# Attention pieces in three steps instead of two: transposes and their copy, then the next scores, then the older product

## The chip, the core and the metric

One NeuronCore of a Trainium2 chip runs one program. Its engines work side by side and wait for each other by semaphores: TensorE (PE in the profile, its weight loads PEld), VectorE (DVE), ScalarE (ACT), GpSimd (POOL) and SyncE (SP, which issues the DMAs). Each engine works off a queue of its own. The metric is the device time of one execution in microseconds (us).

## What is computed

Two transformer blocks, one after the other. The first has two layers over two streams, 256 context and 256 latent tokens of 1024 channels; each layer is a feed-forward part, a mixer (differential attention beside a Fourier mixer, merged by gates) and a second feed-forward part. The second block (gated delta rule, mLSTM, experts) is not touched here. The part that matters is the attention of the first block:

```python
def diff_attend(q, k, v, lam):
    s = jnp.einsum("bqhcd,bkhcd->bhcqk", q, k).astype(jnp.float32) * (HEAD_DIM ** -0.5)
    p = jax.nn.softmax(s, axis=-1)
    a = p[:, :, 0] - lam * p[:, :, 1]
    return jnp.einsum("bhqk,bkhe->bqhe", a.astype(v.dtype), v)
```

There are 8 heads. Each has two score maps c of 64 channels, whose softmaxes are subtracted, and values of 128 channels. Context tokens attend to the 256 context keys, latent tokens to all 512 keys. The last layer computes latent queries alone.

## The kernel before

Matrix products are made of three products each, of high and low halves (mm3, L169 to L171), to keep float32's precision; the weights arrive by DMA as "wraw" and are split on ScalarE and VectorE into "whi" and "wlo" (L140, L141). Such products of weights and tokens are called "pg" in the mixer.

Attention goes by pieces of 128 queries of one head. Layer 0 has 32 pieces, in the order of the heads and, within a head, two context pieces (256 keys) and two latent ones (512 keys). Layer 1 has 16, all of 512 keys. The method `attend` (L527) is a generator; a piece does the following:

- scores: six matmuls into two accumulators "psc" (one for each c)
- softmax: on VectorE the two maxima (L540), on ScalarE the two exponentials "e" with their sums (L542), on VectorE the reciprocal (L544), the scaling (L545) and the difference of the two maps (L546, which writes "e" again). Here the generator yields
- transposes: one for each 128 keys into "pT" on TensorE (L550), with a copy to "aT" by ScalarE (L552)
- the values' product: one matmul for each 128 keys into "po" (L555; the trace shows two records for each) and a copy to "o" by ScalarE (L557).

In the loop of `mixer` (L663 to L680) a piece's first part is recorded, then the rest of the piece before. When a head's last piece is through, `head_done` squares its output ("sqo", ScalarE) and sums it on TensorE into "pst"; after heads 1 and 3 it also records the projections of the next queries and keys (`pair`), and the gates' projections are recorded behind the loop, each held back behind a "pst" (`issue_after`, L683). These projections are the "pg" matmuls that the scheduler puts between the steps of the pieces; they are called fillers below. `split_qk` splits the next head's queries and keys into halves ("qh", "kh" on ScalarE, "ql", "kl" on VectorE).

What is recorded goes through a scheduler. It fills the queue of each engine one instruction at a time, with the earliest recorded one that it takes to be ready at that point; so what stands where between the pieces is its doing, and a change in the order of recording moves fillers and splits too. Buffers set limits: the accumulators "psc", "pT", "po" and "pst" share four ("pa"), the fillers' four others ("ps").

Of the kernel before, what the change touches and what calls it, by code (L numbers as in the profile page):

```python
# [35 lines left out]
class Kernel:  # L36
    def __init__(self, ctx, tc, A, NW=4, NTMP=6):
# [21 lines left out]
        # ones in column s  # L59
# [4 lines left out]
        # picks row 32 g + s into column 2 g + s  # L64
# [6 lines left out]
        # adds the rows 32 g + s into column s  # L71
# [3 lines left out]
    def block(self, n, nch):  # L75
        """Pools of one of the two blocks."""
        st = ExitStack()
        self.act = st.enter_context(self.tc.tile_pool(name=f"act{n}", bufs=nch, reuse_waits="tile"))
        self.bp = st.enter_context(self.tc.tile_pool(name=f"blk{n}", bufs=1, reuse_waits="tile"))
        return st  # L80

    # ---- tiles
# [15 lines left out]
    # ---- small parameters as columns [128, rows]  # L98
# [23 lines left out]
    # ---- weights: raw -> (hi, lo), both exact in float32r  # L122
    def weights(self, src, k0, nk, c0, ncol=256, nsplit=2, half=None):
# [7 lines left out]
        with ExitStack() as order:  # L131
            # the second weights after a norm are not split ahead of it
# [11 lines left out]
    def weights_parts(self, srcs, n):  # L144
        """For several [src, first column] of 8 x 128 rows, 256 columns: their (hi, lo), and functions that load and split the i-th of
        n parts of the rows of each."""
# [26 lines left out]
    # ---- adaLN vectors  # L173
# [10 lines left out]
    def ada(self, cm, wsrc, i, bias, out, streams=(0, 1)):  # L184
        """(A generator; its second step is best taken some time after the first.) out [128, NK, 2] =
        silu(c) @ w[:, i-th D columns] + bias columns, the products on DVE, summed over the partitions on PE."""
# [36 lines left out]
    def ada_quarter(self, cm, ws, q, bias, out):  # L223
        """The channels of the q-th 256 of such a vector, the products on PE, for both streams."""
# [17 lines left out]
    # ---- statistics over the model dimension  # L242
    def square(self, c, s, xt, scales=(None,)):
        """Adds (x * scale)^2 of the chunk c of stream s to the sums of its tokens, for each of scales."""
# [10 lines left out]
    def sums(self, s, i=0):  # L255
        """[128, 256] PSUM (all partitions alike): those sums over the model dimension."""
        pt = self.pa("pst")[:, :S]
        self.nc.tensor.matmul(pt, self.ones, self.sq.pop((s, i)), start=True, stop=True)
        return pt

    def rsqrt_table(self, t):
        """Has the table of rsqrt loaded ahead of its use, once t is there."""
# [5 lines left out]
    def rsqrt(self, sums, n, tag="rs", k=1):  # L268
        """rsqrt(sums / n + k eps), k 1, 4 or eps: the engine's estimate with one Newton step."""
# [16 lines left out]
    def modulated(self, x, gs, sh, streams):  # L286
        """(x * rstd * gs + sh) split into hi, lo; gs, sh [128, NK, 2]."""
# [9 lines left out]
    def norm_part(self, U, x, gs, sh, s, r, cs):  # L297
        """The chunks cs of the stream s of it, into U."""
# [13 lines left out]
    def scale_cols(self, g, sc, name):  # L312
        """g * (1 + scale): [128, NK, 2]."""
# [16 lines left out]
    def ffn(self, x, U, w_in, w_out, gate, streams, fill=lambda end=False: None, scales=(None,), fills=(), head=None):  # L330
# [3 lines left out]
        for a in range(0, nchunk, 8):  # L334
            b = min(a + 8, nchunk)
            H = []
            for j in range(a, b, 2):
# [14 lines left out]
                if j == 0 and head is not None:  # L352
                    begin, end = head(U, load, split)
                    wdma = self.wdma
                    # the vectors' products run ahead of the others by a quarter
# [46 lines left out]
    def load_x(self):  # L402
        """The streams as 8 tiles [128 channels, 256 tokens] each; self.r: their rstd."""
# [33 lines left out]
    # ---- attention / Fourier mixer  # L437
    def mixer_consts(self):
        nc = self.nc
        # ones in column h of the h-th block  # L440
# [20 lines left out]
    def gemm_t(self, src, U, nk, c0, nchunk, sl, done, first=False, tail=(), half=None):  # L461
        """done(m, psum) for each 128-column chunk of src[:, c0:], as [columns, tokens] of the slice sl;
        for the last two chunks done(m, psum, part) for each part of tail."""
# [25 lines left out]
    def gemm_rows(self, src, U, c0, ncol, toks, done, first=False):  # L489
        """done(t, c, psum[:, :256]) for each 128 tokens x 256 columns, as [tokens, columns]."""  # L490
# [36 lines left out]
    def attend(self, h, Q, K, V, lam, q0, nkeys, out):  # L527
        """out [128 e, 128 q] <- head h of the queries from q0 on, keys 0..nkeys; Q, K: its hi, lo."""
# [23 lines left out]
        nc.scalar.copy(aT, pT)  # L552
        po = self.pa("po")[:, :128]
# [5 lines left out]
    def mixer(self, x, U, l, last, lam_init, gcol, bg, gate, fill=lambda end=False: None):  # L559
        """gcol: subln_g column; bg: b_gate columns [128, 16]; gate: [128, NK, 2]."""  # L560
# [50 lines left out]
        # Fourier mixing  # L611
# [5 lines left out]
        # cosines of the frequencies 0..128, sines of 1..127: the others' are these, the sines negated  # L617
# [19 lines left out]
        def gdone(dst, m0):  # L637
            def done(m, p):
                t = self.ch(name="gate")
                # sigmoid(z) = (tanh(z / 2) + 1) / 2, the half taken with w_o's gate  # L640
# [21 lines left out]
        prev = ahead = None  # L662
        for h in range(8):  # L663
# [4 lines left out]
            for s in qstreams:  # L668
                for q0 in (s * S, s * S + 128):
                    u = self.attend(h, *halves, V, lam, q0, T if s == LAT else S, o[:, q0:q0 + 128])  # L670
                    next(u)
                    if prev:
                        next(prev[0], None)
                        if prev[1] is not None:
                            head_done(*prev[1])
                    prev = (u, (h, o) if (s, q0) == (LAT, S + 128) else None)
                    if (s, q0) == (LAT, S) and h + 1 < len(Q):
                        ahead = split_qk(h + 1)
        next(prev[0], None)
        head_done(*prev[1])  # L680
# [39 lines left out]
    # ---- second block: mixer  # L720
# [21 lines left out]
    def final_and_mod(self, X, gs, sh):  # L742
        """hi, lo of the modulated norm of rms_norm(X, fg); gs: its gain, times fg."""
        nc = self.nc
        sq = [self.sq.pop((LAT, i)) for i in range(2)]
        # rsqrt(mean(x1^2) + eps) of x1 = X fg rsqrt(mean(X^2) + eps), times the latter:
        # rsqrt(mean((X fg)^2) + eps (mean(X^2) + eps))
# [11 lines left out]
    def final_norm(self, X, fg, sq):  # L759
        """(A generator of two steps.) X <- rms_norm(X, fg), in place; sq: the sums of its squares by partition."""  # L760
# [8 lines left out]
    def block2_consts(self):  # L769
        nc, A = self.nc, self.A  # L770
        c = self.bp
        # the last to be read lie first
        self.OA, self.OB = (c.tile([128, 2, 8, 64], F32, name="O" + n) for n in "AB")
        self.sqn = c.tile([128, 2, 8], F32, name="sqn")
        # strictly later (fwd) and strictly earlier (rev): [j, i]
# [8 lines left out]
        # per gate row: bias, sign, coefficient  # L784
# [18 lines left out]
    def gate_rows(self, U):  # L803
        """The gates' projections and what the recurrences need of them."""
# [1115 lines left out]
```

## Time and profile before

| | us |
|---|---|
| median of 3 runs | 2866.65 |
| lowest and highest run | 2863.99, 2866.95 |
| span of the profiled execution, first to last instruction | 2863.3 |
| attention stretch of layer 0 (615.1 to 767.6) | 152.5 |
| attention stretch of layer 1 (1789.9 to 1893.9) | 104.0 |

The profiled execution has a span of its own; a run's time is a little more, since it also holds what lies around the span. A start in the rows is counted from the span's start. A matmul's duration overlaps the next one's start, so the cost of one in a row of equals is the distance of two starts. Idle time before an instruction stands in square brackets in a timeline, with the instruction that ended it.

### The profile page before, as it was taken

To read this page: it belongs to the slowest core of one execution; us is meant where nothing else is said; L and a number is where in the kernel's file an instruction comes from. 1 tells how busy PE (TensorE), PEld (TensorE's weight loads), DVE (VectorE), ACT (ScalarE), POOL (GpSimd) and SP (SyncE) were. 2 spreads that over 40 slices of the span, in tenths; PEclk is the share of its full clock that TensorE was granted. 3 is DMA by queue.
4 is the path that set the end of the run, shared out by engine and by line. 5 is a ranking of instruction groups with operands and counts; after the bars stand their busy time and mean duration, and the time that the engine had idled before them with its cause. 6 is when DMAs were issued, how large, how long until landed. Compare 5 with 4: busy or idle time off the path is not lost. (4 is left out here: it accounts for less than half of the span.)

```text
span 2863.3 us, 39743 instructions
## 1 busy us (share of the span) xinstructions
PE 2776.7 (97%) x16186; PEld 2266.0 (79%) x16186; DVE 1726.5 (60%) x2974; ACT 1089.8 (38%) x1994; POOL 28.4 (1%) x97
## 2 busy tenths in 40 slices
PE   8999999999999999999999999999998999999997
PEld 6787789876778777788777899779998898895443
DVE  5855675357558656665464565866567865564332
ACT  4222243335624222242222344555446555543222
POOL 0000000000000000000000000000000100000000
PEclk9999999999999999999999999999999999999999
DMA  7644444131123446436464454234555320159997
GB/s 253 207 146 162 145 146 156 63 105 45 45 89 133 162 147 209 168 126 202 154 215 151 149 172 143 74 104 162 177 175 159 102 74 23 33 192 341 366 366 251
DMA packets 354695, 450.27 MB, mean 157 GB/s; under 512 B 13919, under 2 KB 319945, under 8 KB 354505
## 3 DMA queue, kind: packets, MB, share of 16 engines
q1 hardware_dynamic: 352489, 442.42, 46.8%
q0 software_dynamic: 864, 3.15, 0.3%
q8 instruction: 129, 2.11, 0.3%
q10 hardware_dynamic: 1152, 2.10, 0.2%
q14 instruction: 61, 0.50, 0.1%
HBM read 446.57 MB, written 1.05 MB: 156 GB/s over the span
## 5 line engine op out<-in xcount | busy, mean ns | idle before, releaser
L140 ACT CAST whi<-wraw 128x1024 fp32r<-128x1024 f32 (+2 forms) x476 | 466.1, 1005 | 724.7 <-PE py L170 220.8
L141 DVE TENSOR_TENSOR wlo<-wraw,whi 128x1024 fp32r<-128x1024 f32 (+2 forms) x476 | 548.8, 1168 | 254.2 <-ACT whi L140 251.9
L169 PE MATMUL pab<-uh,whi 128*128 128x512 f32 (+1 forms) x1472 | 527.1, 362 | 8.4 <-ACT uh L307 8.4
L171 PE MATMUL pab<-uh,wlo 128*128 128x512 f32 (+1 forms) x1472 | 528.9, 360 | 0.9 <-DVE wlo L141 0.9
L170 PE MATMUL pab<-ul,whi 128*128 128x512 f32 (+1 forms) x1472 | 529.6, 361 | 0.0
L169 PEld LDWEIGHTS pab<-uh,whi 128*128 128x128 f32 x1472 | 276.9, 190 | 60.5 <-ACT uh L307 9.3
L171 PEld LDWEIGHTS pab<-uh,wlo 128*128 128x128 f32 x1472 | 278.8, 190 | 46.7 <-DVE wlo L141 1.6
L170 PEld LDWEIGHTS pab<-ul,whi 128*128 128x128 f32 x1472 | 279.1, 190 | 44.4 <-DVE ul L308 0.4
L198 DVE SCALAR_TENSOR_TENSOR part<-wada,cm,part 128x1024 f32<-128x1024 f32 x238 | 292.6, 1283 | 19.9 <-DMA wada<-in_ada_w_dram 10.8
L171 PE MATMUL pg<-uh,wlo 128*128 128x256 f32 (+1 forms) x864 | 285.6, 331 | 2.3 <-DVE wlo L141 2.3
L169 PE MATMUL pg<-uh,whi 128*128 128x256 f32 (+1 forms) x864 | 286.2, 332 | 1.5 <-ACT cvo L888 0.9
L170 PE MATMUL pg<-ul,whi 128*128 128x256 f32 (+1 forms) x864 | 285.1, 330 | 0.0
L170 PE MATMUL py<-hl,whi 128*128 128x512 f32 (+1 forms) x740 | 265.1, 358 | 0.1
L169 PE MATMUL py<-hh,whi 128*128 128x512 f32 (+1 forms) x740 | 264.7, 358 | 0.0
L171 PE MATMUL py<-hh,wlo 128*128 128x512 f32 (+1 forms) x740 | 263.7, 357 | 0.0
L169 PEld LDWEIGHTS pg<-uh,whi 128*128 128x128 f32 x864 | 165.6, 192 | 20.4 <-issue 2.8
L171 PEld LDWEIGHTS pg<-uh,wlo 128*128 128x128 f32 x864 | 165.4, 192 | 19.7 <-issue 3.7
L170 PEld LDWEIGHTS pg<-ul,whi 128*128 128x128 f32 x864 | 165.8, 192 | 14.6 <-issue 1.9
L169 PEld LDWEIGHTS py<-hh,whi 128*128 128x128 f32 x740 | 139.0, 188 | 23.8 <-issue 1.2
L170 PEld LDWEIGHTS py<-hl,whi 128*128 128x128 f32 x740 | 139.2, 188 | 22.7 <-DVE hl L380 0.3
L171 PEld LDWEIGHTS py<-hh,wlo 128*128 128x128 f32 x740 | 139.1, 188 | 22.7 <-issue 0.4
L377 DVE TENSOR_TENSOR silu<-silu,pab 128x512 f32<-128x512 f32 (+1 forms) x88 | 54.3, 620 | 144.5 <-PE pab L171 144.3
(494 smaller groups left out, 4233.4 us busy)
## 6 DMA issues: line engine op xcount, KB each, us to landing
wraw<-in_ffn_w_in_dram SPq DMA_DIRECT2D x86, 1024.0 KB
wraw<-in_w_in_dram SPq DMA_DIRECT2D x68, 1024.0 KB
wada<-in_w_mod_dram SPq DMA_DIRECT2D x64, 1024.0 KB
wraw<-in_ffn_w_out_dram SPq DMA_DIRECT2D x32, 1024.0 KB
wm<-in_w_gate_dram SPq DMA_DIRECT2D x61, 512.0 KB
wm<-in_w_up_dram SPq DMA_DIRECT2D x61, 512.0 KB
wm<-in_w_down_dram SPq DMA_DIRECT2D x30, 1024.0 KB
wada<-in_ada_w_dram SPq DMA_DIRECT2D x24, 1024.0 KB
```

Of the source, the lines that this page charges most:

```text
L140: nc.scalar.copy(hi[:, a:b], raw[:, a:b])
L141: nc.vector.tensor_tensor(lo[:, a:b], raw[:, a:b], f32(hi[:, a:b]), op=OP.subtract)
L169: nc.tensor.matmul(ps, wh, uh, start=first, stop=False)
L170: nc.tensor.matmul(ps, wh, ul, start=False, stop=False)
L171: return nc.tensor.matmul(ps, wl, uh, start=False, stop=last)
L198: nc.vector.scalar_tensor_tensor(p, w[:, k], c, p, op0=OP.mult, op1=OP.add)
L377: nc.vector.tensor_tensor(t[:, sl], t[:, sl], P[2 + i], op=OP.mult)
```

## The change

The generator yields a second time, between the copy "aT" and the values' product. The loop keeps a list of pieces that are not through. For each new piece it first records the transposes and the copy of the piece before it, then the new piece's scores and softmax, then the product of the piece before last. At the end of the layer the last transposes are recorded and the products that are left. Comments are taken out elsewhere, so lines behind L552 have a number one higher, and behind the loop nine higher.

```diff
@@ attend
         aT = self.tmp(name="aT")[:, :nkeys]
         nc.scalar.copy(aT, pT)
+        yield
         po = self.pa("po")[:, :128]
...
@@ mixer
-        prev = ahead = None
+
+        ahead, pieces = None, []
+
+        def third():
+            u, end = pieces.pop(0)
+            next(u, None)
+            if end is not None:
+                head_done(*end)
         for h in range(8):
             o = self.ch(name="o")
             O.append(o)
...
                     u = self.attend(h, *halves, V, lam, q0, T if s == LAT else S, o[:, q0:q0 + 128])
+                    if pieces:
+                        next(pieces[-1][0])
                     next(u)
-                    if prev:
-                        next(prev[0], None)
-                        if prev[1] is not None:
-                            head_done(*prev[1])
-                    prev = (u, (h, o) if (s, q0) == (LAT, S + 128) else None)
+                    pieces.append((u, (h, o) if (s, q0) == (LAT, S + 128) else None))
+                    if len(pieces) == 3:
+                        third()
                     if (s, q0) == (LAT, S) and h + 1 < len(Q):
                         ahead = split_qk(h + 1)
-        next(prev[0], None)
-        head_done(*prev[1])
+        next(pieces[-1][0])
+        while pieces:
+            third()
```

The built programs hold the same instructions but for two table loads of ScalarE, which the new order has more, and differ in order in the two attention stretches alone; the DMA issues stand as before. Three places show it. The numbers behind the names tell buffers apart.

TensorE, near the end of layer 1, before: the transposes of a piece, its own product, the next scores.

```order
L169 MATMUL psc_14584<-kh_14547,qh_14543 128x512
L170 MATMUL psc_14584<-kl_14548,qh_14543 128x512
L171 MATMUL psc_14584<-kh_14547,ql_14544 128x512
L169 MATMUL psc_14588<-kh_14547,qh_14543 128x512
L170 MATMUL psc_14588<-kl_14548,qh_14543 128x512
L171 MATMUL psc_14588<-kh_14547,ql_14544 128x512
L550 MATMUL pT_14601<-ident_67,e_14561 128x128 x4
L555 MATMUL po_14608<-aT_14606,v_12421 128x128
```

The same place after:

```order
L550 MATMUL pT_14577<-ident_67,e_14559 128x128 x4
L169 MATMUL psc_14585<-kh_14538,qh_14534 128x512
L170 MATMUL psc_14585<-kl_14539,qh_14534 128x512
L171 MATMUL psc_14585<-kh_14538,ql_14535 128x512
L169 MATMUL psc_14589<-kh_14538,qh_14534 128x512
L170 MATMUL psc_14589<-kl_14539,qh_14534 128x512
L171 MATMUL psc_14589<-kh_14538,ql_14535 128x512
L556 MATMUL po_14602<-aT_14547,v_12421 128x128
L556 MATMUL po_14602<-aT_14547,v_12423 128x128
L556 MATMUL po_14602<-aT_14547,v_12425 128x128
L556 MATMUL po_14602<-aT_14547,v_12427 128x128
L550 MATMUL pT_14608<-ident_67,e_14594 128x128 x4
```

Before, the transposes behind a piece's scores belong to the piece before it, and the product to those transposes. After, the transposes read the softmax of the scores just above them (e_14594 comes from psc_14585), with one older product between.

ScalarE at that place, before: two exponentials, then the copy.

```order
L542 ACTIVATE e_14593,st_14583<-psc_14584,st_14583 128x512
L542 ACTIVATE e_14596,st_14583<-psc_14588,st_14583 128x512
L552 COPY aT_14606<-pT_14601 128x512
L557 COPY o_14508<-po_14608 128x128
L657 ACTIVATE sqo_14614<-o_14508 128x256
```

After:

```order
L552 COPY aT_14582<-pT_14577 128x512
L542 ACTIVATE e_14594,st_14584<-psc_14585,st_14584 128x512
L542 ACTIVATE e_14597,st_14584<-psc_14589,st_14584 128x512
L558 COPY o_14502<-po_14602 128x128
L552 COPY aT_14613<-pT_14608 128x512
```

The copy of the transposes has moved from behind the next piece's exponentials to ahead of them.

TensorE in layer 0, at the end of head 5's and in head 6's pieces, before: fillers between a piece's transposes and its product.

```order
L550 MATMUL pT_5853<-ident_67,e_5818 128x128 x2
L169 MATMUL pg_6107<-uh_3115,whi_6100 128x512
L170 MATMUL pg_6107<-ul_3116,whi_6100 128x512
L171 MATMUL pg_6107<-uh_3115,wlo_6101 128x512
L169 MATMUL pg_6108<-uh_3073,whi_6100 128x512
L170 MATMUL pg_6108<-ul_3074,whi_6100 128x512
L171 MATMUL pg_6108<-uh_3073,wlo_6101 128x512
L169 MATMUL pg_6108<-uh_3079,whi_6100 128x512
L170 MATMUL pg_6108<-ul_3080,whi_6100 128x512
L171 MATMUL pg_6108<-uh_3079,wlo_6101 128x512
L169 MATMUL pg_6108<-uh_3085,whi_6100 128x512
L555 MATMUL po_5858<-aT_5856,v_3179 128x128
```

After, between two pieces of head 6:

```order
L550 MATMUL pT_5831<-ident_67,e_5814 128x128 x2
L169 MATMUL psc_5837<-kh_5734,qh_5730 128x512
L170 MATMUL psc_5837<-kl_5735,qh_5730 128x512
L171 MATMUL psc_5837<-kh_5734,ql_5731 128x512
L169 MATMUL psc_5841<-kh_5734,qh_5730 128x512
L170 MATMUL psc_5841<-kl_5735,qh_5730 128x512
L171 MATMUL psc_5841<-kh_5734,ql_5731 128x512
L556 MATMUL po_5854<-aT_5802,v_3179 128x128
L556 MATMUL po_5854<-aT_5802,v_3181 128x128
L550 MATMUL pT_5866<-ident_67,e_5846 128x128 x4
```

The fillers that stood here have moved to earlier pieces. Counted from one piece's scores to the next's, layer 0 has, before: 2, 15, 10, 14, 15, 6, 10, 7, 0, 7, 19, 11, 6, 2, 12, 12, 27, 8, 10, 13, 6, 2, 10, 12, 6, 2, 10, 8, 6, 2, 9 and 61 fillers; after: 17, 11, 15, 18, 7, 5, 6, 0, 0, 0, 28, 15, 7, 9, 13, 16, 7, 1, 32, 15, 9, 6, 15, 13, 6, 0, 0, 0, 0, 0, 5 and 64. Layer 1, before: 0, 35, 13, 8, 9, 58, 14, 9, 15, 51, 26, 14, 5, 0, 0, 45; after: 28, 18, 11, 8, 0, 4, 48, 12, 11, 21, 46, 18, 25, 7, 0, 45. The "pst" of a head stands two pieces into the next head after, one piece before.

## Rows read from the trace of the kernel before

**Rows 1.** The page: busy us, share of the span, instructions.

```profile
PE 2776.7 (97%) x16186; PEld 2266.0 (79%) x16186; DVE 1726.5 (60%) x2974; ACT 1089.8 (38%) x1994; POOL 28.4 (1%) x97
```

**Rows 2.** Windows of both attention stretches: length, busy by engine, clock, DMA share, GB/s.

```profile
615.10:767.60 152.50, 146.06 (x795) 102.40 (x794) 106.42 (x229) 92.01 (x248) 0.00 (x0) 0.99 0.15 49
1789.90:1893.90 104.00, 96.33 (x579) 72.70 (x577) 75.44 (x149) 60.83 (x146) 0.00 (x0) 0.95 0.22 72
```

**Rows 3.** Waits, whole span: who for whom, us in total, times, longest.

```profile
PEld po L555 <- ACT aT L552: 25.4, 35, 2.4
PE po L555 <- ACT aT L552: 12.0, 16, 2.1
PE pT L550 <- DVE e L546: 0.4, 2, 0.2
```

**Rows 4.** Timeline, TensorE, layer 1, no fillers: start, us, instruction, idle before.

```profile
1876.20 0.50 PE L169 MATMUL psc<-kh,qh 64*128 64x512 f32 x2
...
1879.90 1.16 PE L555 MATMUL po<-aT,v 128*128 128x128 f32 x8 [2.14 <-ACT aT L552]
1880.99 0.50 PE L169 MATMUL psc<-kh,qh 64*128 64x512 f32 x2
```

**Rows 5.** Timeline, VectorE, the same piece.

```profile
1877.20 1.29 DVE L540 TENSOR_REDUCE st<-psc 128x1 f32<-128x512 f32 x2 [0.92 <-PE psc L171]
...
1880.18 0.75 DVE L546 SCALAR_TENSOR_TENSOR e<-e,st 128x512 f32<-128x512 f32 x1
```

**Rows 6.** Timeline, ScalarE, the same stretch.

```profile
1879.26 0.58 ACT L552 COPY aT<-pT 128x512 f32<-128x512 f32 x1
```

**Rows 7.** Timeline, TensorE, layer 0, a piece of 256 keys.

```profile
746.84 0.39 PE L169 MATMUL psc<-kh,qh 64*128 64x256 f32 x2
...
747.40 0.66 PE L550 MATMUL pT<-ident,e 128*128 128x128 f32 x4
```

**Rows 8.** Timeline, VectorE, the same piece: the softmax's last step.

```profile
749.73 0.48 DVE L546 SCALAR_TENSOR_TENSOR e<-e,st 128x256 f32<-128x256 f32 x1
```

**Rows 9.** Timeline, TensorE, layer 0: product, scores, transposes and fillers.

```profile
645.64 0.71 PE L555 MATMUL po<-aT,v 128*128 128x128 f32 x4 [0.41 <-ACT aT L552]
646.28 0.50 PE L169 MATMUL psc<-kh,qh 64*128 64x512 f32 x2
...
647.18 0.66 PE L550 MATMUL pT<-ident,e 128*128 128x128 f32 x4
647.59 0.48 PE L171 MATMUL pg<-uh,wlo 128*128 128x512 f32 x1
...
648.14 0.39 PE L170 MATMUL pg<-ul,whi 128*128 128x512 f32 x1
648.37 0.40 PE L171 MATMUL pg<-uh,wlo 128*128 128x512 f32 x1
```

**Rows 10.** Timeline, TensorE, layer 0: the sum of squares of a head.

```profile
751.82 1.05 PE L658 MATMUL pst<-sqo,hcol 128*32 128x512 f32 x2
752.80 0.49 PE L170 MATMUL pg<-ul,whi 128*128 128x512 f32 x1
```

**Rows 11.** Windows, TensorE alone: length, busy, granted clock, DMA share, GB/s.

```profile
650.00:660.00 10.00, 7.90 (x41) 0.83 0.33 105
1876.20:1882.00 5.80, 3.66 (x23) 0.95 0.53 177
1882.00:1892.00 10.00, 8.98 (x35) 0.52 0.00 0
```

**Rows 12.** Timeline, VectorE, layer 0: a softmax with a weight split in it.

```profile
680.61 1.29 DVE L540 TENSOR_REDUCE st<-psc 128x1 f32<-128x512 f32 x2 [0.79 <-PE psc L171]
683.08 1.23 DVE L141 TENSOR_TENSOR wlo<-wraw,whi 128x1024 fp32r<-128x1024 f32 x1 [1.18 <-ACT whi L140]
...
685.00 0.75 DVE L546 SCALAR_TENSOR_TENSOR e<-e,st 128x512 f32<-128x512 f32 x1
```

**Rows 13.** Groups by line, ScalarE, 766 to 780 us: busy, mean ns, idle before.

```profile
L280 ACT ACT_TABLE_LOAD x1 | 1.3, 1283 | 0.0
```

## The prediction

> **What bounds the kernel now.** I read the page first: TensorE is busy 97% of the span [rows 1], so whatever TensorE loses or gains is time. Next the windows around the two attention stretches, the only places where the order of instructions differs: 152.5 us in layer 0 and 104.0 us in layer 1, in which TensorE is idle 6.4 and 7.7 us and its clock is granted nearly in full [rows 2]. Then the waits: the values' product "po" waits for the copy "aT", 12.0 us in all, 16 times, and its weight loads 25.4 us, 35 times; a transpose "pT" hardly ever waits for the softmax, 0.4 us [rows 3]. Last the timelines of pieces.
>
> The reader should see one thing in them. Every piece has two delays off TensorE: the softmax on VectorE and ScalarE, and the copy of the transposes on ScalarE. Before, TensorE has the previous piece's transposes and product and the next piece's scores to do while the softmax of a piece runs, and covers it; the copy stands behind the next piece's two exponentials in ScalarE's queue, and that is the bound where no filler is at hand: scores at 1876.20, next scores at 1880.99, a period of 4.79 us, 2.14 us of it a wait for the copy [rows 4, 6].
>
> **The change, part by part.** No arithmetic is added. *Removed:* the wait for the copy. The copy now stands ahead of the exponentials, and its product comes one period later. What goes is between 12.0 us (idle matmuls) and 25.4 us (idle weight loads) [rows 3], since the load that waits also delays the matmul behind it; I take 20, nearer to the loads, because a product's first weight load is waited for in full after each stop.
>
> *Added:* a wait of the transposes for the softmax. After the change only the product of the piece before last (and filler) lies between a piece's scores and its own transposes. What a softmax needs, with nothing else on its engines: 512 keys, from the scores at 1876.20 to the end of the last VectorE step, 1880.18 + 0.75 = 1880.93, is 4.73 us [rows 4, 5], plus 0.1 for the hand-over (the copy ends at 1879.84, its product starts at 1879.90 [rows 4, 6]), less the scores' own 0.90 (646.28 to 647.18 [rows 9]): 3.9 us to be covered. 256 keys: 746.84 to 749.73 + 0.48 = 750.21, so 3.37 + 0.1 - 0.56 = 2.9 us [rows 7, 8]. What covers: a product of four weight blocks, 1879.90 to 1880.99, 1.09 us [rows 4]; of two, 645.64 to 646.28, 0.64 us; each filler of 512 columns 0.23 us (648.14 to 648.37) [rows 9], and I take half for those of 256; the sum "pst" 0.98 us (751.82 to 752.80 [rows 10]) in layer 0, half in layer 1.
>
> Now the fillers of the new order, piece by piece (numbers from 0). Layer 0, the bare and nearly bare pieces: 6 is short by 3.9 - 0.64 - 1.4 = 1.9; 7, 26 and 27 by 3.9 - 0.64 = 3.3 each; 8 and 28 by 2.9 - 1.09 = 1.8 each; 9, 25 and 29, with a "pst", by 2.9 - 1.09 - 0.98 = 0.8 each; 17 by 1.6; 30 by 2.1. Together 21.5 us. The others have 5 to 32 fillers (5 and 21, with 5 and 6, also a "pst") and are covered but for 0.2 to 0.4 us in seven of them: 1.9 us. Layer 1: pieces 4 and 14 (no filler) 2.8 each, 15 2.3 (its 45 fillers come after the last transposes), 5 1.8, 13 1.5; five others 1.2 in all: 12.4 us. So 23.4 + 12.4 = 36 us, on softmaxes with nothing in their way.
>
> Many have something in their way: splits of weights, queries and keys stand between the steps of a softmax, now as before. The nearest row is a 512-key softmax with such a split (683.08, 1.23 us) inside: from its maxima at 680.61 to 685.00 + 0.75 it takes 5.14 us, against 3.73 in the clean one (1877.20 to 1880.93) [rows 5, 12]. That is 1.4 more. About half of the uncovered pieces have one in the new order, so 0 to 14 us; I take 7. New waits: 43 us (36 to 50).
>
> *The clock.* Before, it is 0.83 in the ten us around 650 to 660 and 0.52 in 1882 to 1892 [rows 11], that is 3.4 and 9.6 us at 1.2 GHz, both after pieces without filler. Now layer 0 has six nearly bare periods in a row (25 to 30, some 27 us). If all of them ran at 1.2 GHz, the scores and transposes on the chain (0.90 + 0.41 for 512 keys) would double (0.41 is 647.18 to 647.59 [rows 9]): 6 x some 1.2 = 7 us. If the level holds, 0. I take 3, since a run of bare periods from 1866.5 on still had 0.95 in 1876.2 to 1882 and lost the level after that [rows 11]. The Trainium skill, "TensorE: Matmul & The Clock Gate", section "A second HAM failure mode: psum-queue depth-cycling", says that an array which idles briefly and often between groups of matmuls swings between its two clock levels and pays at each swing. By that rule the whole 7 us would be due and the sum 4 us higher; the granted clock of 0.52 after short waits agrees with it.
>
> *Hidden.* The change also has two more table loads on ScalarE behind the last piece of layer 0, 1.3 us each [rows 13]. Some 70 fillers of 0.23 us, 16 us, stand on TensorE there before anything needs ScalarE's result, in either order; without them the loads would cost 2.6 us. The product of a piece needs one of the four "pa" accumulators, of which "pst" and two scores hold three: it then waits for the copy that empties the fourth, which runs while the scores do (0.58 us [rows 6] against 0.56 to 0.90 [rows 7, 9]): nothing, or 0.1 us in a few pieces. Loads of weights are issued in the same order as before. After attention everything is the same row of work on a busy TensorE, so a delay goes through to the end.
>
> *Sum:* -20 + 36 + 7 + 3 = +26 us. On the profiled execution that is a span of 2863.3 + 26 = 2889 us; the median of the runs is 3.3 us above that span, and 2866.65 + 26 = 2893 us.
>
> **A check by chains.** Without filler a 512-key period becomes 4.73 + 0.1 and 0.41 for the transposes ahead of the next scores, 5.2 us and more against 4.79 now [rows 4, 5, 9]; a 256-key one 3.37 + 0.1 + 0.3 = 3.8 [rows 7, 8]. A head of layer 0 (two of each) then has a chain of at least 18 us, eight heads 145. The stretch's own work on TensorE is 152.5 less its share of the 20 us (32 of 48 pieces, 13), some 139 us. So the softmax's chain passes TensorE's work, and the mean filler no longer helps unless it lies evenly, which it does not.
>
> **Rivals.** (a) *Faster.* The removed wait is all that counts, because the bare periods are covered by something that I call uncovered. Each of the 16 bare or nearly bare pieces costs 1 to 3.3 us, 33 us together, 2 on average; if fewer than ten of them wait, the removed 20 us win. With none waiting: 2866.65 - 20 = 2847. For it: before, even bare periods show no wait for the softmax [rows 3]. Against: there the next scores and a whole copy and product stood in between [rows 4]. Chance 0.05. (b) *Cancelling.* Removed at its upper bound, 25.4, new waits a quarter below theirs, 27, no clock: +2, 2869. For it: the fillers' first matmul after a change of tile takes more than 0.23 us, which covers more. Chance 0.06. (c) *More.* Removed at its lower bound of 12, softmaxes with all of the 14 us in their way, clock 7: -12 + 50 + 7 = +45, 2912. For it: the splits of the next head's queries and keys now fall inside the softmaxes of pieces 2, 6, 22 and 26. Chance 0.12. (d) *The change is not done:* the built order shows it on both engines, so none. The forecast has the rest, 0.77.
>
> **How the numbers follow.** A measurement of this kernel can tell about 0.2%, 5.7 us, from no change. The forecast's own ends are +9 (-25.4 + 36 - 2) and +45; leaving a tenth on either side, 2875 to 2911. Slower 0.77 + 0.12 = 0.89, within 0.06, faster 0.05.
>
> **What would show it.** In the profile after: "po" waiting for "aT" near zero; "pT" waiting for "e" up from 0.4 to some 25 to 40 us; the stretch of layer 0 about 18 us longer, that of layer 1 about 7; pieces 25 to 30 of layer 0 with waits of 1 to 3.5 us at each transpose and a granted clock below 1 there; the rest of the kernel as it was, shifted. Wrong would be the step on coverage if the transposes of those pieces start at once, and the step on the removed waits if "po" still waits.

## The result and the profile after

The changed kernel takes 2905.18 us (median of 4 runs, 2900.53 to 2905.39), the kernel before 2866.32 beside it (2863.99 to 2866.95): a ratio of 1.0133, 95% interval 1.0120 to 1.0146. That is 39 us more, where 26 were forecast; the time lies inside the range. The spans of the profiled executions are 2903.7 and 2863.3 us, 40.4 apart, of which 1.7 us lie ahead of the first scores. Below, "the first stretch" and "the second" are the attention of layer 0 and of layer 1.

The page of after, the line that answers [rows 1]:

```profile
PE 2795.1 (96%) x16186; PEld 2280.2 (79%) x16186; DVE 1727.0 (59%) x2974; ACT 1092.9 (38%) x1996; POOL 28.4 (1%) x97
```

The same instructions keep TensorE busy 18 us longer than in [rows 1]: either they are held up more, or the engine's clock is lower. The windows of both stretches, from the first scores to the last sum of squares, answer [rows 2] (length, busy us by engine, clock, DMA share, GB/s):

```profile
616.70:802.90 186.20, 161.52 (x792) 112.45 (x791) 106.92 (x229) 92.82 (x247) 0.00 (x0) 0.86 0.12 40
1824.90:1934.50 109.60, 97.60 (x575) 74.56 (x574) 75.99 (x149) 60.75 (x146) 0.00 (x0) 0.91 0.21 68
```

Here the 39 us split in two. TensorE's *idle* time is length less busy: 24.7 and 12.0 us, against 6.4 and 7.7 in [rows 2], so 18.3 + 4.3 = 22.6 us more. Its *busy* time is 161.5 and 97.6 us against 146.1 and 96.3: 16.7 us more, nearly all in the first stretch, at a granted clock of 0.86 instead of 0.99. In the second stretch the clock is 0.91 instead of 0.95, for 1.3 us of busy time. Between the stretches (1022.0 us, before 1022.3) and behind them (969.2, before 969.4) nothing changed.

Who waits for whom in after, answering [rows 3] (us in total, times, longest):

```profile
PE pT L550 <- DVE e L546: 25.0, 20, 3.9
PE pst L659 <- ACT sqo L658: 8.2, 9, 1.8
...
PE pg L169 <- ACT gate L642: 1.9, 1, 1.9
...
PE po L556 <- ACT aT L552: 0.5, 2, 0.3
```

The wait of the product "po" for the copy "aT", 12.0 us before, has gone but for 0.5. In its place the transposes wait for the softmax, and two waits are there that no step of the prediction had: the sum of squares "pst" for the square, and the gates' fillers for an accumulator.

TensorE at the transposes of piece 6, the last ahead of the first run of bare pieces, and in the bare pieces 26 to 29 of the first stretch (start, us, instruction, idle before and what ended it), answering [rows 4, 7]:

```profile
652.18 1.09 PE L550 MATMUL pT<-ident,e 128*128 128x128 f32 x4 [2.52 <-DVE e L546]
...
765.95 1.08 PE L550 MATMUL pT<-ident,e 128*128 128x128 f32 x4 [3.91 <-DVE e L546]
766.97 0.80 PE L169 MATMUL psc<-kh,qh 64*128 64x512 f32 x2
...
768.55 1.22 PE L556 MATMUL po<-aT,v 128*128 128x128 f32 x4
772.70 1.09 PE L550 MATMUL pT<-ident,e 128*128 128x128 f32 x4 [2.94 <-DVE e L546]
...
774.66 2.07 PE L556 MATMUL po<-aT,v 128*128 128x128 f32 x8
777.55 0.66 PE L550 MATMUL pT<-ident,e 128*128 128x128 f32 x2 [0.82 <-DVE e L546]
...
782.17 1.91 PE L659 MATMUL pst<-sqo,hcol 128*32 128x512 f32 x2 [1.01 <-ACT sqo L658]
784.01 0.69 PE L550 MATMUL pT<-ident,e 128*128 128x128 f32 x2
```

The waits stand where the forecast put them. But the work between them is slow too: four transposes take 1.1 us instead of 0.66 [rows 7], a product of eight 2.07 instead of 1.16 [rows 4], "pst" 1.91 instead of 1.05 [rows 10]. VectorE in piece 27, answering [rows 5]: it is no slower than before, and TensorE starts 0.14 us after its last step (771.81 + 0.75 = 772.56).

```profile
768.65 1.29 DVE L540 TENSOR_REDUCE st<-psc 128x1 f32<-128x512 f32 x2 [2.24 <-PE psc L171]
...
771.81 0.75 DVE L546 SCALAR_TENSOR_TENSOR e<-e,st 128x512 f32<-128x512 f32 x1
```

TensorE's clock around the two runs of bare pieces in after (length, busy, granted clock, DMA share, GB/s), answering [rows 11]:

```profile
651.60:672.10 20.50, 15.19 (x58) 0.50 0.16 51
764.30:795.00 30.70, 22.43 (x81) 0.50 0.00 1
```

For 51.2 us the engine runs at 1.2 GHz; before, 3.4 us of the first stretch did. Each time the clock falls inside a wait of the transposes (649.7 to 652.2, and 762.0 to 766.0 us). It comes back at 672.1 and 795.0 us, when TensorE has run without a wait since 668.4 and 789.3. Of the 37.6 us busy there half, 18.8, is what the lower level costs if all of it were on the path; 15.5 us of longer busy time was measured in this stretch.

### The profile page after: what moved, and what is told of

Read it like the earlier page. It is cut to its first block, busy times and chain, and to the rows that moved or that the text cites. A ratio compares the mean times of both kernels' runs of the same rounds, so it can differ in the third digit from the quotient of the medians.

```text
span 2903.7 us, 39740 instructions
## 1 busy us (share of the span) xinstructions
PE 2795.1 (96%) x16186; PEld 2280.2 (79%) x16186; DVE 1727.0 (59%) x2974; ACT 1092.9 (38%) x1996; POOL 28.4 (1%) x97
## 3 DMA queue, kind: packets, MB, share of 16 engines
HBM read 446.57 MB, written 1.05 MB: 154 GB/s over the span
## 5 line engine op out<-in xcount | busy, mean ns | idle before, releaser
L170 PEld LDWEIGHTS pg<-ul,whi 128*128 128x128 f32 x864 | 165.6, 192 | 15.5 <-issue 2.2
L170 PEld LDWEIGHTS py<-hl,whi 128*128 128x128 f32 x740 | 139.3, 188 | 22.6 <-DVE hl L380 0.3
L171 PEld LDWEIGHTS py<-hh,wlo 128*128 128x128 f32 x740 | 139.3, 188 | 22.6 <-issue 0.4
```

The lines of the kernel that those rows point to most:

```text
L170: nc.tensor.matmul(ps, wh, ul, start=False, stop=False)
L171: return nc.tensor.matmul(ps, wl, uh, start=False, stop=last)
```

## The experiments

All times are medians. The kernel before was run beside each and gave 2866.3 to 2867.0 us; ratios are to it.

**The softmax in the transposes' way.** Three steps of each softmax are left out, in the changed kernel and, as a control, in the kernel before. The transposes then read the first of the two exponentials:

```
-        nc.vector.reciprocal(st[:, 4:6], st[:, 2:4])
-        nc.vector.tensor_scalar(E[1], E[1], st[:, 5:6], lam, op0=OP.mult, op1=OP.mult)
-        nc.vector.scalar_tensor_tensor(E[0], E[0], st[:, 4:5], E[1], op0=OP.mult, op1=OP.subtract)
```

> The changed kernel without three steps of each softmax: the reciprocal, the scaling of the second exponential and the difference (L545, L546, L547 of before) are left out, and the transposes read the first exponential. The path from a piece's scores to its transposes is shorter by these three: 0.17 + 0.41 + 0.48 = about 1.1 us with 256 keys and 0.17 + 0.55 + 0.74 = about 1.5 us with 512, and nothing that TensorE does changes. Theory (the transposes wait for the end of the softmax): of the 24.9 us of waits of pT over 0.2 us some 16 go (18.0 in the first stretch become about 6, 6.8 in the second about 2.6), and with them part of the time at 1.2 GHz: 2872 to 2886 us, a fall of 20 to 33, several times that of the kernel before with the same steps left out. Rival (the later order costs through something other than the length of the softmax: the sums' product, the fillers' places, the tile changes on TensorE): 2898 to 2906, a fall no larger than that of the kernel before.

> The kernel before without the same three steps of each softmax (reciprocal, scaling, difference), the transposes reading the first exponential. Theory (in the order of before a piece's transposes come a whole piece after its scores, so the softmax has been done by then: only one wait of pT over 0.2 us, of 0.24, stands in its trace; its waits are for the copy aT): nearly nothing to gain, 2860 to 2867 us. Rival (the softmax bounds the bare pieces of before too, by VectorE's and ScalarE's busy time): 2845 to 2858.

Changed kernel: 2864.66 us (2859.99 to 2867.05), 40.5 less than with the whole softmax. Kernel before: 2860.38 (2859.55 to 2862.73), 6.3 less. The changed kernel fell further than the theory said, the control to the low edge of what it allowed. The waits of the shortened changed kernel, then those of the shortened kernel before:

```profile
PE pT L547 <- ACT e L542: 2.0, 6, 0.4
```

```profile
PE po L552 <- ACT aT L549: 8.7, 19, 2.1
```

The transposes' waits are down from 25.0 us to 2.0, no time at 1.2 GHz is left in either stretch, and of the 39 us between the two orders 4.3 are left between the shortened ones. So the softmax in front of the transposes is what the new order exposes. How much of it was taken away is another matter. The expectation says three steps, 1.1 to 1.5 us; but with the first exponential alone to read, the transposes no longer wait for the second map's maximum and exponential either. In the shortened changed kernel the transposes of a piece start before its second exponential does (ScalarE, TensorE, ScalarE):

```profile
718.40 0.69 ACT L542 ACTIVATE e<-psc,st 128x512 f32<-128x512 f32 x1 [0.85 <-DVE st L540]
719.98 0.60 PE L547 MATMUL pT<-ident,e 128*128 128x128 f32 x4
720.86 0.69 ACT L542 ACTIVATE e<-psc,st 128x512 f32<-128x512 f32 x1
```

In piece 27 of the changed kernel the first exponential ends at 770.07 us and the last step of the softmax at 772.56: some 2.5 us of 3.9 left the path, which is why the time fell further than the theory said. The scheduler also set another order: the stretches hold fewer fillers, and a piece's second three scores often stand behind fillers or a "pst". So only the totals are compared; they show the cause, not a price for each us of softmax.

**The clock.** Ahead of the transposes of pieces 7 to 9 and 25 to 29 of the first stretch, TensorE does eight matmuls whose result the transposes overwrite:

```
+        for _ in range(8 if junk else 0):
+            nc.tensor.matmul(pT, K[0][:, :128], K[0][:, :nkeys], start=True, stop=True)
```

> The changed kernel with eight useless matmuls (128 keys of weights, as many columns as the piece has keys) into the accumulator of the transposes ahead of these, in the eight pieces of layer 0 that have no filler (7 to 9, 25 to 29); the transposes overwrite them. About 1.9 or 0.9 us of work each at 2.4 GHz, 12 us together, all of it in waits. Clock theory (a good part of the loss in layer 0 is TensorE at 1.2 GHz, in 651 to 672 and 764 to 795 us): the granted clock stays at 2.4 GHz there and the kernel gets faster though it does more, by 8 to 14 us: 2891 to 2897 us. Rival (the waits alone are the loss, the clock is a companion): same or slower, 2905 to 2912 us.

2895.71 us (2893.54 to 2902.28): 9.5 us less than the changed kernel, with 11.8 us more work on TensorE; the ranges of the two just overlap. Windows of its two stretches:

```profile
615.80:793.20 177.40, 163.96 (x856) 115.41 (x855) 107.04 (x229) 92.40 (x247) 0.00 (x0) 0.97 0.13 42
1816.90:1926.60 109.70, 97.68 (x576) 74.48 (x574) 75.99 (x149) 60.75 (x146) 0.00 (x0) 0.91 0.21 68
```

The first stretch is 8.8 us shorter at a clock of 0.97, with 10.2 us at 1.2 GHz instead of 51.2; the second, left alone, is as it was. Busy time rose by 2.4 us only, though 11.8 were added, so the work that was there already ran 9.4 us faster. That the clock is a price of its own is shown by that; 9.4 us is what it gave back in busy time, as far as this kernel took the lower level away.

Idle time went from 24.7 to 13.4 us, 11.3 less, and there the run is less clean than its text says. In the eight pieces the scheduler also put the next piece's scores, whole or in part, ahead of the transposes; in piece 26:

```profile
759.53 2.07 PE L550 MATMUL pT<-kh 128*128 128x512 f32 x8
761.53 0.50 PE L169 MATMUL psc<-kh,qh 64*128 64x512 f32 x2
...
763.37 0.66 PE L552 MATMUL pT<-ident,e 128*128 128x128 f32 x4 [0.88 <-DVE e L546]
```

So the shorter waits come from the added work and from these scores together, and what the added work alone would have made of the time is not shown.

**Fillers spread.** The gates' fillers, which the kernel releases behind heads 3, 3, 5 and 7, are released behind 3, 4, 5 and 6:

```
-        for h in (3, 3, 5, 7):
+        for h in (3, 4, 5, 6):
```

> The changed kernel with the gates' projections, the last fillers, released behind the sums of heads 3, 4, 5 and 6 instead of 3, 3, 5 and 7. In layer 0 the built order then has the bare pieces 21 and 27 to 29 in place of 25 to 29, and the same work. Clock theory: a run of three bare pieces loses the clock for a shorter time than one of five, a gain of 4 to 10 us: 2895 to 2901 us. Rival (a bare piece costs the same wherever it stands): within 2 us of the changed kernel, 2903 to 2907 us.

2900.76 us, but from 2897.26 to 2910.45; the profiled run was the longest, with a span of 2908.7 us and its second stretch 4 us longer. Its first stretch, where the bare pieces were moved, has 41.0 us at 1.2 GHz instead of 51.2 and is 1.1 us shorter. Inconclusive: the median says the one, its spread allows the other.

**The product not delayed.** The product comes one piece earlier, the transposes stay ahead of the next scores:

```
-                    if len(pieces) == 3:
+                    if len(pieces) == 2:
```

> The product of a piece is recorded right behind the next piece's scores, not one piece later; transposes and copy still go ahead of the scores. Theory (the chain scores, softmax, transposes, next scores sets the pace of bare pieces): this chain is as in the changed kernel and the cover is one product either way, so 2897 to 2909 us, 30 to 42 us above the kernel before, with the transposes waiting for the softmax some 25 us as in the changed kernel. Rival (the later product costs, since the head's sum and the fillers that wait for it come a piece later): at least half of the loss goes, 2872 to 2886 us.

2898.76 us (2893.27 to 2900.09), ratio 1.0110 (1.0093 to 1.0127). Its waits:

```profile
PE pT L550 <- DVE e L546: 18.6, 19, 3.0
...
PE pst L659 <- ACT sqo L658: 8.8, 8, 1.8
```

Another 4.5 us of the transposes' waits are put down to a cast of keys on ScalarE ("kh"), in two places where the softmax ended only 0.15 us before the transposes began (758.07 and 758.23 us; 1898.73 and 1898.88). So they wait nearly as long as in the changed kernel, and TensorE's idle time in the two stretches is no less, 37.4 us against 36.7. What is less is the time at the lower clock: 27.3 us of the first stretch are at 1.2 GHz instead of 51.2. This kernel differs from the one before in that transposes stand ahead of the next scores, with the fillers moved by it, and that costs 32 of the 39 us; the later product adds the rest, and the trace shows it as busy time, not as waits.

**The wait of "pst".** Each head's square and its product are taken one piece later:

```
+            while sums:
+                head_done(*sums.pop())
             if end is not None:
-                head_done(*end)
+                sums.append(end)
```

> The changed kernel with each head's square and its product into pst taken one piece later, so that ScalarE has long copied and squared the head's outputs when TensorE comes to that product. In the changed kernel these products wait 8.2 us in nine places, and the next piece's transposes stand behind them (781.83 us softmax done, 784.01 us transposes). Theory (pst's wait is a price of its own): the waits of pst fall to under 1 us and the time by 3 to 8 us, to 2897 to 2902. Rival (TensorE would wait for the softmax anyway, so the wait only moves to pT): pT's waits rise by as much and the time stays at 2903 to 2907.

2901.68 us (2898.58 to 2905.71), and a miss in its premise: "pst" waits longer, 13.0 us instead of 8.2, since the square now stands behind two more exponentials on ScalarE:

```profile
PE pT L550 <- DVE e L546: 20.6, 19, 4.0
PE pst L659 <- ACT sqo L658: 13.0, 10, 2.7
```

Then with the square issued at once and only the product later:

```
+            while sums:
+                head_done(*sums.pop())
             if end is not None:
-                head_done(*end)
+                sums.append(head_square(*end))
```

> The changed kernel with each head's product into pst taken one piece later, but its square still issued right behind the copy of the head's outputs (with both moved, the square came behind the next two exponentials on ScalarE, and pst waited longer, 13.0 us instead of 8.2). Theory (pst's wait is a price of its own): pst waits under 1.5 us in all, and 2896 to 2902 us. Rival (TensorE then waits for the softmax in pT instead): pT rises by 5 us or more, and 2902 to 2907 us.

2903.02 us (2899.97 to 2904.22):

```profile
PE pT L550 <- DVE e L546: 22.2, 15, 3.4
PE pst L662 <- ACT sqo L658: 5.3, 8, 1.3
PE pg L169 <- ACT rp L585: 4.9, 3, 1.9
PE pg L169 <- ACT gate L642: 2.4, 1, 2.4
```

"pst" and "pT" wait 2.9 and 2.8 us less than in the changed kernel (but 1.0 us of waits of "pT" is put down to "whi" here), the fillers "pg" 5.4 more. Neither theory: the wait moved to a third place. Both runs overlap with the changed kernel's; what "pst" alone costs stays open.

**Scores first.** One more yield in the piece, so that TensorE does the next piece's scores, then the transposes and copy of the piece before, and its product once the softmax is issued:

```
             P.append(p)
+        yield
         E = []
...
+                    next(u)
                     if pieces:
                         next(pieces[-1][0])
...
-                    if len(pieces) == 3:
+                    if len(pieces) == 2:
```

> The scores of a piece are recorded first, then the transposes and the copy of the piece before, then the softmax, then the product of the piece before. ScalarE has the copy ahead of the exponentials, as in the changed kernel, but the scores stand ahead of the transposes, as before. Theory: a softmax of 512 keys, 3.9 us, then has behind it the older transposes 0.41, the wait for the copy 0.7, the product 1.1 and the next scores 0.9, together 3.1; a bare period takes 3.9 to 4.0 us against 4.8 before and 5.3 or more after, less than TensorE's own work per piece. So faster than before by most of the waits for the copy: 2846 to 2858 us. Rival (to take the copy ahead of the exponentials delays the softmax and costs by itself): no gain, 2866 us or more.

2866.40 us (2862.01 to 2868.57, 10 runs), ratio 0.9999 (0.9990 to 1.0009): a miss. The waits did go:

```profile
PE po L557 <- ACT aT L553: 3.1, 6, 0.8
PE pT L551 <- DVE e L547: 3.0, 6, 1.0
```

and the second stretch is 3.5 us shorter than before, but the first is 9.3 us longer. There the scores are slow. First the six score matmuls of a 512-key piece in the changed kernel, then in this one:

```profile
625.91 0.51 PE L169 MATMUL psc<-kh,qh 64*128 64x512 f32 x2
...
626.48 0.41 PE L171 MATMUL psc<-kh,ql 64*128 64x512 f32 x2
```

```profile
645.52 0.48 PE L171 MATMUL pg<-uh,wlo 128*128 128x512 f32 x1
645.93 0.50 PE L169 MATMUL psc<-kh,qh 64*128 64x512 f32 x1
...
646.41 0.50 PE L169 MATMUL psc<-kh,qh 64*128 64x512 f32 x1
...
646.98 0.39 PE L171 MATMUL psc<-kh,ql 64*128 64x512 f32 x1
```

The two halves of a head use 64 rows each and normally run in pairs, 0.01 us apart ("x2"). From the start of the matmul ahead of them (625.71) to the start of the last of the six (626.49) that is 0.78 us; this measure is used below too. Here the second half starts 0.48 us behind the first, and from 645.52 to 646.98 it is 1.46 us: 0.68 more, of which 0.48 are this delay and 0.2 a later start of the first half. ScalarE in this kernel, just before:

```profile
646.14 0.21 ACT L543 ACTIVATION_READ_ACCUMULATOR e<-psc,st 128x1 f32 x1
```

It reads the last piece's second half out of its accumulator until 646.35, 0.06 us before the late half starts. So measured, and without the fillers between them, the scores of the first stretch take 31.4 us in all, against 22.1 before: 9.3 us more. That is the size of the stretch's excess, but not all that changed: TensorE is busy 11.3 us longer there and idle 2.0 us less, with 10.2 us at 1.2 GHz instead of 3.4. The Trainium skill, "TensorEngine Tiling (Array Packing)", section "Tiling Modes", says that tiles of part of the rows work independently, each on its own matmul. The "x2" rows agree, and the second fence shows the gain lost when one half has no accumulator.

Whether it is the accumulator was tested with a fourth one for the pieces: each head's sums go into a "pa" tile that VectorE adds up and gives back.

```
-        pst = self.pa("pst")
+        acc = {s: self.hf(name="hsum")[:32] for s in qstreams}
...
+            p = self.pa("pst")
+            ends.append(nc.tensor.matmul(p[:32, qsl], self.hcol[:, h, :], sq[:, qsl], start=True, stop=True))
...
+                    nc.vector.tensor_tensor(acc[s], acc[s], ph, op=OP.add)
...
-            r = self.rsqrt(pst[:32, s * S:(s + 1) * S], 128)
+            r = self.rsqrt(acc[s], 128)
```

> The order of the run with the next piece's scores first, in both mixers, but the sums of squares of each head go into an accumulator of their own, which VectorE adds to a tile of its own and gives back, so that the pieces have four accumulators of the pool and not three. In that run the six score products of a piece began one after another in many pieces (1.45 us with 512 keys, 0.81 with 256, against 0.79 and 0.56 side by side; 31.4 us in all of the first stretch, 22.1 before), the second three behind the end of the last piece's second exponential. Theory (the accumulator that this exponential still reads is what holds them): the sum of the first stretch falls to 22 to 25 us, the stretch to 152 to 156 us, and the time to 2856 to 2863 us. Rival (they lose their overlap through the order itself, or VectorE's added sums cost as much): 2865 to 2869 us, the sum above 29.

2884.77 us (2879.45 to 2887.07): a miss by 20 us, for a reason that neither theory had. The scores of 512 keys did what the theory said: up to 747 us, in the heads that have fillers, ten of the twelve pieces take 0.78 to 0.82 us and two 1.2, where the run before had 1.05 to 1.53 in most. Those of 256 keys did not: 9.2 us in these heads, 8.3 in the run before and 7.4 in the kernel before; why is open. The sum of the first stretch fell to 28.3 us, not to 22 to 25, and in the second stretch from 16.8 to 13.9. And the five pieces from 25 on lost their fillers, which went to earlier pieces, and there the waits came back:

```profile
PE pT L551 <- DVE e L547: 14.1, 20, 3.0
PE pst L661 <- ACT sqo L659: 7.7, 5, 2.6
```

with 30.7 us of the stretch at 1.2 GHz. The waits have the names of the changed kernel's, but their chain is another, since here the next scores do stand ahead of the transposes. ScalarE, VectorE and TensorE in two bare pieces:

```profile
762.00 0.59 ACT L553 COPY aT<-pT 128x512 f32<-128x512 f32 x1 [5.22 <-PE pT L551]
```

```profile
758.09 0.69 DVE L541 TENSOR_REDUCE st<-psc 128x1 f32<-128x512 f32 x1 [4.11 <-PE psc L171]
...
759.93 0.75 DVE L547 SCALAR_TENSOR_TENSOR e<-e,st 128x512 f32<-128x512 f32 x1
```

```profile
760.83 1.09 PE L551 MATMUL pT<-ident,e 128*128 128x128 f32 x4 [2.76 <-DVE e L547]
```

In VectorE's queue the last steps of a softmax stand behind the next piece's maximum, which waits for the next scores; the exponentials had been done since 756.6 us. In ScalarE's queue the next exponentials (762.49) stand behind the copy, which waits for the transposes. So a bare piece's softmax is held by its neighbours, which is the rival of the run before, seen at last in the pieces without filler. An order that suits a piece with fillers fails in one without.

**The part that gained, alone.** The first mixer as before, the second with scores first (against the kernel with scores first in both):

```
                     next(u)
+                    if not last:
+                        next(u)
                     if pieces:
                         next(pieces[-1][0])
-                    next(u)
+                    if last:
+                        next(u)
```

> The first mixer in the order of before; the second mixer alone (16 pieces of 512 keys) with the next piece's scores first, then the transposes and copy of the piece before, then its product once the softmax has been issued. Theory (in the run with that order in both mixers the second stretch was 3.5 us shorter than before, and the first longer by some 5 without its fillers, since there two score products of 64 rows no longer ran side by side): the first stretch as before, 151 to 153 us, the second 100 to 101 instead of 103.6, and the time 2862 to 2864 us. Rival (the shorter second stretch is paid back behind it, or was clock of one execution): 2865.5 to 2867.5.

2862.86 us (2859.68 to 2866.87, 11 runs), ratio 0.9985 (0.9976 to 0.9994). Its two stretches:

```profile
615.00:767.60 152.60, 146.16 (x795) 102.42 (x794) 106.41 (x229) 92.14 (x248) 0.00 (x0) 0.99 0.15 49
1789.40:1889.90 100.50, 96.17 (x585) 72.63 (x584) 75.05 (x149) 60.12 (x146) 0.00 (x0) 1.00 0.23 74
```

The first is that of before, the second has 4.3 us idle instead of 7.7 and the full clock. With the accumulator given back in the second mixer as well:

```
+            p = self.pa("pst") if last else pst
+            ends.append(nc.tensor.matmul(p[:32, qsl], self.hcol[:, h, :], sq[:, qsl], start=last or h == 0, stop=last or h == 7))
```

> The kernel with the order of before in the first mixer and the scores first in the second, with the accumulator of the sums given back in the second mixer as well. There only six of sixteen pieces had their score products one after another (16.8 us in all against 15.8 before), so theory and rival are near: theory 2860 to 2863 us (the second stretch 98.5 to 100), rival (VectorE's eight added sums of 256 columns on the way, and six fillers moved away from every second piece): 2863 to 2866.

2861.84 us (2855.14 to 2866.59, 11 runs), ratio 0.9982 (0.9973 to 0.9991), second stretch 99.3 us in the profiled run, which was the shortest. Both are a little faster than the kernel before, by 0.15 and 0.18%; the two can't be told from each other.

## Why the prediction was right, and where it was not

Direction and mechanism held, by the chain of the prediction: the wait for the copy goes, a larger one for the softmax comes, it falls on the pieces without filler, and what follows is shifted. The size was 13 us short, and the time came nearer to the rival "more" (2912 us) than to the forecast (2893).

*Removed waits: mis-sized.* 20 us were taken, between 12.0 and 25.4. Idle TensorE fell from 12.0 us to 0.5 there, so the lower bound was the value; what the weight loads waited beyond that did not come back as idle time. The reason given for the upper half, that a product's first weight load is waited for in full, is not borne out.

*Added waits: right in their places, too large in sum.* 43 us were taken; 25.0 + 8.2 + 1.9 = 35.1 came. For the bare pieces the working was close: 3.3 us each for pieces 7, 26 and 27, and 2.9, 3.9 and 2.9 were measured; 1.9 for piece 6 and 2.5; 1.8 for pieces 8 and 28 and 0.8 each, because at half the clock the product that covers lasts twice as long. Piece 17 had 1.6 and 1.4. "pst" was counted as 0.98 us of cover. It covers nothing where it waits itself: ScalarE first copies and squares the head's outputs,

```profile
781.19 0.27 ACT L558 COPY o<-po 128x128 f32<-128x128 f32 x1 [0.53 <-PE po L556]
781.49 0.63 ACT L658 ACTIVATE sqo<-o 128x512 f32<-128x512 f32 x1
```

"pst" starts at 782.17 after a wait of 1.0 us, and the transposes behind it at 784.01, their softmax long done on VectorE (781.34 + 0.48 us). Piece 30's 2.1 us came as 1.9 us of another kind, fillers that wait for the gates. Splits inside softmaxes were given 7 us; in pieces 6 and 26, where they should show, the softmax takes 4.4 us from its first maximum, in piece 27 without a split 3.9. The forecast of 1.4 for each was too much. In the second stretch 12.4 us were forecast, and 6.8 us for the softmax and 4.7 us at "pst" came.

*The two errors cancelled, by luck:* 43 - 20 = 23 us was the forecast of the net wait, and 22.6 us more of idle time was measured.

*The clock: the term that was mis-sized, and nearly all of the 13 us.* 3 us were taken out of 0 to 7; TensorE was busy 16.7 us longer, and in the clock experiment 9.4 us of it came back with the clock. Two things were wrong in the step. It counted one run of bare pieces, 25 to 30, while pieces 6 to 9 lost the clock as well (651.6 to 672.1 us). And it doubled only scores and transposes, since the product and "pst" were taken as cover that costs nothing. At half the clock they too were on the path: after a wait, all that TensorE does before its next wait is. The row that was leaned on, 0.95 in 1876.2 to 1882 [rows 11], was one of short waits ending in a lower level, and was read as a level that holds. The rule that the prediction takes from the Trainium skill, "TensorE: Matmul & The Clock Gate", section "A second HAM failure mode: psum-queue depth-cycling", pointed the right way. This trace agrees with it in part: in the first stretch the clock did not swing from wait to wait but fell twice and stayed low for 20.5 and 30.7 us, and the 7 us put to the rule were too few.

*Hidden:* right. ScalarE has four table loads from 801.75 us on where it had two, and what follows on TensorE is not longer (1022.0 us to the second stretch, before 1022.3).

*By stretch:* some 18 us were forecast for the first and 7 for the second; 33.7 and 5.6 came. The first's idle time alone rose by 18.3, so its excess is the 15.5 us of busy time, and the clock is the one cause of that which the runs show. *The chains:* a bare 512-key period was given as 5.2 us and more, and is 6.75 at the lower level (765.95 to 772.70).

*The range:* its lower end, 9 us, holds a further 2 us taken off for which no row is given; it did not matter here.

*The rivals:* "faster" and "cancelling" fell with the first bare piece. "More" had the right sign of the clock, 7 us, but its other parts, 14 us of splits and only 12 removed, were half right: 12 was the removed wait, and the splits cost little.

## What to carry to other kernels

A software-pipelined loop should keep the longer of its off-engine delays behind the larger block of TensorE work: here the softmax (3.9 us) lost the next scores and a copy's wait as its cover, to free a copy that cost 12 us in all. Look at the queues of the other engines as well: with the scores ahead again, the softmax was held behind the next maximum and the copy. Price an order at its poorest iterations, those without filler, not at the mean, and count as cover only work that does not wait for something itself. Where the trace shows the clock down after such iterations, as before the change in the second stretch [rows 11], price everything between their waits at the lower clock. And when a run is made to test one cause, read its built order first: the scheduler moved scores in two of these.

## What the runs showed of the hardware that was not expected

The granted clock fell inside a wait of 2.5 us and one of 3.9 us, and stayed at 1.2 GHz for 20.5 and 30.7 us, with 15.2 and 22.4 us of work in them; it came back in stretches in which TensorE did not wait. With eight useless matmuls in each bare piece, 11.8 us in all, and the next scores partly ahead of the transposes, 10.2 us at that level were left and the kernel was 9.5 us faster.

Two matmuls of 64 rows each ran side by side, 0.01 us apart, and six of them took 0.78 us. When one half started 0.48 us behind the other, for want of an accumulator, the six took 1.46 us. No row of TensorE's waits shows it, since the engine was busy with the other half.
